# A different turn of gate quads, a later place for the transposes of u, earlier norms, and six weight tiles for five in a hybrid recurrence and retention layer

## The chip, the cores and the metric

The kernel runs on one core of a Trainium2 chip. The metric is device time in microseconds. The engines are TensorE (PE; its weight loads are PEld), VectorE (DVE), ScalarE (ACT), GpSimd (POOL) and SyncE (SP). Each works through its own instructions in order and waits for the others on semaphores. ACT, SP and POOL also issue DMA transfers; in the profile such issues stand under ACTq, SPq and POOLq.

## The reference

One layer over 2048 positions of width 1024, in float32:

```
h   = rms_norm(x) * (1 + scale(c)) + shift(c)
P   = h @ W_in         # 1024 x 9216: q f i z | q k v z | gA gB
uA  = headRMSNorm(HGRN2(q, f, i)) * silu(zA)
uB  = headRMSNorm(Retention(rot(q), rot(k), v)) * silu(zB)
m   = sigmoid(gA) * uA + sigmoid(gB) * uB
out = rms_norm(x + gate(c) * (m @ W_out))
```

Both branches have 8 heads. HGRN2 is a recurrence with a decay for each key channel: S_t = diag(f_t) S_(t-1) + (1 - f_t) i_t^T, o_t = S_t^T q_t. Retention has one fixed decay for each head and rotary positions on q and k.

## The kernel before

The sequence is worked on in two halves (superblocks) of 1024 positions, each as two blocks of 512. All columns of W_in for one head and purpose form a "quad": a 2 x 2 arrangement of two column groups by the two blocks. Each quad is computed by Strassen's scheme with Winograd's sums, so with seven products (numbered 1 to 7) in place of eight, and each product is four steps of three matmuls: every operand is split into a high and a low part in a reduced float32 format (fp32r), and high x high, high x low and low x high are added. A step is thus three matmuls of 128 x 512.

There are 36 quads in a half. Their names in the table ORDER are a (HGRN2 q and f of a head), v (both branches' values), b (retention q and k of a head pair), A and B (the gates zA with gA, and zB with gB, of a head). `product_order` interleaves the seven products of neighbouring quads: 2 of the new, 7 of the old, 1 and 5 of the new, 4 of the old, 3 and 6 of the new. PE's instructions are kept in the order in which the program writes them; the others are ordered by the scheduler, with priorities.

Results lie in PSUM banks: x0 and x1 in turn for a quad's x (and its y), v for products 5 and 3, lv, two of "o" and one double bank rt for the background. ACT copies y and v out of PSUM (L480); DVE adds or subtracts x (L493, L500, L504).

The raw weights come in tiles of 128 x 512 floats, with DMA issues on ACT's queue (L404), into a ring of NR tiles; DVE forms Winograd's sums in place (L419), and ACT and DVE split them (L293, L294) into the parts that PE reads, three products ahead. A new load is issued when a raw tile is done with.

Everything else is background: Python generators that issue a little work at each turn. `Background.tick` counts product steps; each 8 steps (GAP) all lanes get a turn (a burst), and each 4 steps the "side" generators do. The lanes are, for each head, the tree of score levels (bank lv, L70 with 128x16 and larger outputs, DVE L782 to L794), the HGRN2 output chunks (`hgrn_out`, banks poh), and for each head pair the retention chunks (`retention`, banks por and rt). Both end in `normed`: squares on ACT (L833), a power on POOL (L173 to L176), scaled copies on ACT (L836). The results u go to DRAM (L841). On the side run `next_h` (the normalized input of the second half) and, in the second half, `ada_row` (the gate row).

A quad A or B loads its u from DRAM (`fetch_u`, L670), turns it on PE by four transposes (`turned_u`, L73, tile uT) into bank v for the first block and into a used x bank for the second (`meet_last`), and DVE multiplies (L708). `fetch_u` demands that u has been stored for a while; where it has not, it issues bursts, one behind another, until it has.

`next_h` reads rows of x into two of the five shared temporaries (tag tp), squares them on ACT (L1038), adds on DVE (L1040), takes the power on POOL (L176), scales an identity on POOL (L1043, tile dgr), and has PE multiply by ones (tile rb); then it scales the transposed x. Rotary tables (ct, sn; issued on POOL's queue, L630 and L632) use the same temporaries, as do many results of DVE.

Of the kernel before, what the change touches and what calls it, by code (L numbers as in the profile page):

```python
# [9 lines left out]
F32 = mybir.dt.float32  # L10
# [12 lines left out]
P = 128  # L23
# [7 lines left out]
CH = SB // P  # L31
NA = 28
NBW = 3
NR = 5
NCC = 5
NTP = 5
NQP = 3
NVH = 2
GAP = 8.0
FIRST = 2  # L40


ORDER = """a0 v0 b0 v1 a1 b1 v2 a2 A0 B0 v3 a3 A1 B1 v4 b2 a4 A2 B2 v5 a5 A3 B3 v6 b3 a6 A4 B4 v7 a7 A5 B5 B6 A6 B7 A7"""


def all_quads():
# [3 lines left out]
QUADS = all_quads()  # L50
# [12 lines left out]
def tile_hybrid(ctx: ExitStack, tc: tile.TileContext, a: dict, out: bass.AP):  # L63
# [124 lines left out]
    class Background:  # L188

        def __init__(self):  # L190
            self.lanes = []
            self.side = []
            self.late = []
            self.since = 0.0
            self.beat = 0.0
            self.now = 0.0
            self.posts = []
# [41 lines left out]
        def tick(self, w):  # L239
            self.since += w  # L240
            self.beat += w
            self.now += w
            self.deliver()
            if self.beat >= 4.0:
                self.beat = 0.0
                self.aside()
            if self.since >= GAP:
                if self.burst():
                    self.since = 0.0

# [212 lines left out]
    def product_step(ps, m, q, j, first, last):  # L463
        sb = QUADS[q][0]
        at = combos[sb, ACOMBO[m], j]
        bt = W.parts[m, q]
        at_j = j % 2 * 2 + j // 2
        ls = [z[:, at_j * P : (at_j + 1) * P] for z in bt]
        for n, (x, y) in enumerate(((0, 0), (0, 1), (1, 0))):
            PE.matmul(  # L470
                out=ps, lhsT=ls[x], rhs=at[y], start=first and n == 0, stop=last and n == 2,
                skip_group_check=True,
            )
# [40 lines left out]
    def product(i):  # L514
        m, q = seq[i]
        if m == 2:
            ps = yb[q] = bank(f"y{q}", xtag(q))
        elif m == 1:
            ps = xb[q] = bank(f"x{q}", xtag(q))
        elif m == 5:  # L520
            ps = vb[q] = bank(f"v{q}", "v")
        elif m == 3:
            ps = vb[q]
        else:
            ps = xb[q]
        W.pump(i + NBW)
        for j in range(4):
            product_step(ps, m, q, j, m in (1, 2, 5) and j == 0, j == 3)
            bg.tick(1.0)
        W.parts.pop((m, q))  # L530
        after(m, q)
# [396 lines left out]
    def retention(p, sb):  # L928
# [26 lines left out]
        while n <= CH:  # L955
# [35 lines left out]
                        out=pos[j], lhsT=scms[m][:, j], rhs=vb_[j], start=g == 0, stop=True, skip_group_check=True  # L991
                    )
            if n < CH:
                scms[n] = upool.tile([P, 2, P], F32, name=f"scm{p}_{g0 + n}", tag="scm", bufs=2)
                V.tensor_tensor(out=scms[n], in0=pt[:, :, 0:P], in1=dT.rearrange("p (j t) -> p j t", j=2), op=ALU.mult)
                kzs[n] = upool.tile([P, P], F32, name=f"rkz{p}_{g0 + n}", tag="rkz", bufs=2)
                for j, r in enumerate(rows):
                    S.activation(out=kzs[n][:, r], in_=kz[:, r], func=AF.Copy, scale=zeta[:, h0 + j : h0 + j + 1])
            if n:
                if g and not last:  # L1000
                    V.scalar_tensor_tensor(
                        out=rs, in0=rs, scalar=gC[:, p : p + 1], in1=x, op0=ALU.mult, op1=ALU.add
                    )
                elif g == 0:
                    V.tensor_copy(out=rs, in_=x)
                b = g // 4
                if m % 2 == 0:
                    for j in range(2):
                        u[j] = upool.tile([P, 2, P], F32, name=f"ur{h0 + j}_{g}", tag="ur", bufs=4)
                normed(pos, [u[j][:, m % 2, :] for j in range(2)], f"r{p}_{g}", epsx[:, h0 : h0 + 2])  # L1010
                if m % 2:
                    for j in range(2):
                        send_u(1, h0 + j, b, m % 4, u[j])
                if m == CH - 1:
                    rnext[0] = (sb, p + 1) if p + 1 < NP else (sb + 1, 0)
                    if not last:
                        nc.sync.dma_start(out=rstd_d[p], in_=rs)
# [7 lines left out]
    def next_h(sb):  # L1025
        for tb in range(NBLK):
            b = sb * NBLK + tb
            rb = upool.tile([P, 512], F32, name=f"rb{b}", tag="mu", bufs=4)
            for t in range(4):
# [11 lines left out]
                rstd_of(r[:, 0:1], r[:, 0:1], D)  # L1041
                dg = tmp(f"dgr{b}_{t}", P)
                G.tensor_scalar(out=dg, in0=ident, scalar1=r[:, 0:1], scalar2=None, op0=ALU.mult)  # L1043
                yield
                yield
                ps = bank(f"rb{b}_{t}", "lv")
                PE.matmul(out=ps[:, 0:P], lhsT=ones, rhs=dg, start=True, stop=True)
                S.activation(out=rb[:, t * P : (t + 1) * P], in_=ps[:, 0:P], func=AF.Copy)
# [187 lines left out]
    def ada_row(j):  # L1236
# [9 lines left out]
                V.scalar_tensor_tensor(out=acc, in0=w, scalar=sc[:, kt : kt + 1], in1=acc, op0=ALU.mult, op1=ALU.add)  # L1246
        bgt = tmp(f"bg{j}")
        nc.sync.dma_start(out=bgt, in_=a["bgate"][:, j * 512 : (j + 1) * 512].broadcast_to([P, 512]))
        for _ in range(2):
            yield  # L1250
        ps = bank(f"gps{j}", "lv")
        PE.matmul(out=ps, lhsT=ones, rhs=acc, start=True, stop=True)
# [80 lines left out]
    for i in range(2, len(seq)):  # L1333
        m, q = seq[i]
        kind = QUADS[q][1]
        if m == 6 and 0 in waits:
            meet_last()
        if kind in "AB" and m == 6:
            turned_u(QUADS[q][2], "AB".index(kind), 0, "v")
        if kind in "AB" and m in (2, 1):  # L1340
            fetch_u(q, 2 - m)
        if kind == "b" and m == 2:
            load_rot(q, 0)
        if m == 2 and QUADS[q - 1][1] == "b":
            load_rot(q - 1, 1)
        if QUADS[q] == (0, "a", 5) and m == 1:
            bg.side.append(next_h(1))
        if QUADS[q] == (1, "a", 5) and m == 1:
            bg.side.append(chain(ada_row(0), ada_row(1)))
        if (m, q) == (1, mid):  # L1350
            pro["h"] = change_h(1)
# [130 lines left out]
```

## Time and profile before

| | |
|---|---|
| median of 3 runs | 2147.56 us (2147.33 to 2149.09) |
| the profiled execution | 2156.3 us, its span 2154.3 us |
| PE busy | 1978.3 us, 92% of the span |
| weight loads (PEld) | 1598.5 us, 74% |
| DVE busy | 1416.6 us, 66% |
| ACT busy | 995.0 us, 46% |
| POOL busy | 278.5 us, 13% |
| mean granted clock of TensorE | 0.966 |
| DMA | 259.95 MB in all, 121 GB/s on the mean |

In the page and in the answers of the trace, a line names a group of instructions or a stretch of time: a timeline row has start, duration, engine, line of the program, operation, out<-in (buffer numbers left out), the count, and in brackets the idle time before it and what ended it. A row of the table of stretches has start and end, length, the busy time of PE, PEld, DVE, ACT and POOL with their counts, the granted clock of TensorE as a share of full speed, the busy share of the 16 DMA engines, and GB/s. A row of the waits has the waiting engine, tile and line, the one waited for, the total, the times, and the longest. The chain is the work that ended last, followed back.

### The profile page before, as it was taken

To read this page: it belongs to the slowest core of one execution; us is meant where nothing else is said; L and a number is where in the kernel's file an instruction comes from. 1 tells how busy PE (TensorE), PEld (TensorE's weight loads), DVE (VectorE), ACT (ScalarE), POOL (GpSimd) and SP (SyncE) were. 2 spreads that over 40 slices of the span, in tenths; PEclk is the share of its full clock that TensorE was granted. 3 is DMA by queue.
4 is the path that set the end of the run, shared out by engine and by line. 5 is a ranking of instruction groups with operands and counts; after the bars stand their busy time and mean duration, and the time that the engine had idled before them with its cause. 6 is when DMAs were issued, how large, how long until landed. Compare 5 with 4: busy or idle time off the path is not lost.

```text
span 2154.3 us, 40023 instructions
## 1 busy us (share of the span) xinstructions
PE 1978.3 (92%) x15108; PEld 1598.5 (74%) x15108; DVE 1416.6 (66%) x2677; ACT 995.0 (46%) x2434; POOL 278.5 (13%) x514
## 2 busy tenths in 40 slices
PE   3889799998999879989998999999999899899998
PEld 2668587786777668768787788787777678687887
DVE  4876667675857557657876666676767576568432
ACT  5624444544355345445634445543454345444331
POOL 1001210211022110210002110211021101210000
PEclk9989999999999999989999999999999999899999
DMA  8145424352245536544544424352445324336442
GB/s 288 35 105 126 114 82 107 89 131 81 77 135 154 145 109 171 177 131 146 165 104 121 123 62 111 95 135 74 106 129 148 104 71 108 89 106 180 157 148 87
DMA packets 453120, 259.95 MB, mean 121 GB/s; under 512 B 171712, under 2 KB 406208, under 8 KB 452928
## 3 DMA queue, kind: packets, MB, share of 16 engines
q1 hardware_dynamic: 286752, 172.89, 28.6%
q10 hardware_dynamic: 153120, 76.04, 12.4%
q0 software_dynamic: 13056, 8.47, 1.5%
q8 instruction: 119, 1.95, 0.4%
q14 instruction: 73, 0.60, 0.1%
HBM read 188.03 MB, written 69.21 MB: 119 GB/s over the span
## 4 chain that ended last, share of the span: by engine, by line
PE 43%; DVE 7%; DMA 5%; ACT 4%; POOL 2%; issue 2%; ACTq 0%; SPq 0%; POOLq 0%; DVEq 0%
PE x L70 16%; PE v L70 8%; PE ops L70 8%; PE y L70 3%; DVE b L294 2%; PE lv L70 2%; PE poh L70 2%; PE rt L70 1%; DMA w<-in_w_d_dram 1%; ACT b L293 1%; DVE w L419 1%; PE uT L73 1%; PE por L70 1%; POOL rrh L176 1%; ACT c L480 1%
## 5 line engine op out<-in xcount | busy, mean ns | idle before, releaser
L294 DVE TENSOR_TENSOR b<-w,b 128x512 fp32r<-128x512 f32 (+1 forms) x553 | 346.5, 634 | 279.3 <-ACT b L293 273.7
L293 ACT ACTIVATE b<-w 128x512 fp32r<-128x512 f32 (+1 forms) x553 | 316.7, 583 | 289.6 <-PE x L70 210.2
L70 PE MATMUL x<-A,b 128*128 128x512 f32 x1704 | 429.8, 401 | 12.4 <-ACT c L480 11.5
L70 PE MATMUL v<-S,b 128*128 128x512 f32 x1704 | 429.8, 401 | 8.5 <-ACT c L480 6.0
L70 PE MATMUL x<-S,b 128*128 128x512 f32 x1704 | 431.6, 403 | 1.6 <-DVE c L500 0.9
L70 PEld LDWEIGHTS x<-A,b 128*128 128x128 f32 x1704 | 321.5, 192 | 81.8 <-ACT c L480 12.6
L70 PEld LDWEIGHTS v<-S,b 128*128 128x128 f32 x1704 | 322.0, 192 | 79.7 <-ACT c L480 8.7
L70 PEld LDWEIGHTS x<-S,b 128*128 128x128 f32 x1704 | 321.5, 193 | 68.2 <-DVE c L500 1.3
L419 DVE TENSOR_TENSOR w<-w,w 128x512 f32<-128x512 f32 x284 | 195.1, 687 | 62.7 <-DMA w<-in_w_a_dram 24.4
L70 PE MATMUL y<-A,b 128*128 128x512 f32 x840 | 209.1, 398 | 8.6 <-DVE vt L592 8.6
L70 PEld LDWEIGHTS y<-A,b 128*128 128x128 f32 x840 | 156.9, 190 | 41.8 <-issue 7.4
L70 PE MATMUL ops<-wo,m 128*128 128x512 f32 x768 | 174.8, 389 | 0.0
L70 PEld LDWEIGHTS ops<-wo,m 128*128 128x128 f32 x768 | 144.0, 188 | 30.2 <-DVE m L299 0.4
L173 POOL TENSOR_SCALAR ssh<-ssh 128x1 f32<-128x1 f32 x128 | 44.9, 351 | 845.0 <-ACT uh L833 841.7
L480 ACT ACTIVATE c<-v 128x512 f32<-128x512 f32 x142 | 84.5, 595 | 121.7 <-PE v L70 106.9
L836 ACT ACTIVATE uh<-poh,rrh 128x128 f32<-128x128 f32 x128 | 47.1, 368 | 125.1 <-POOL rrh L176 123.7
L70 PEld LDWEIGHTS lv<-q,k 128*32 128x32 f32 (+1 forms) x5888 | 71.0, 110 | 43.9 <-issue 27.8
L70 PE MATMUL lv<-q,k 128*32 128x16 f32 (+2 forms) x5888 | 82.5, 189 | 18.9 <-DVE ad L794 6.2
L500 DVE TENSOR_TENSOR c<-c,x 128x512 f32<-128x512 f32 x71 | 48.7, 687 | 76.7 <-PE x L70 76.5
L782 DVE TENSOR_TENSOR q<-q,f 128x512 f32<-128x512 f32 x112 | 76.9, 687 | 22.6 <-PE lv L70 22.2
L176 POOL TENSOR_TENSOR rrh<-ssh,mhalf 128x1 f32<-128x1 f32 x128 | 84.0, 656 | 10.4
L783 DVE TENSOR_TENSOR k<-k,f 128x512 f32<-128x512 f32 x112 | 77.1, 688 | 0.0
(191 smaller groups left out, 2409.3 us busy)
## 6 DMA issues: line engine op xcount, KB each, us to landing
w<-in_w_d_dram ACTq DMA_DIRECT2D x128, 256.0 KB
w<-in_w_c_dram ACTq DMA_DIRECT2D x66, 256.0 KB
mu<-ud SPq DMA_DIRECT2D x64, 256.0 KB
w<-in_w_a_dram ACTq DMA_DIRECT2D x60, 256.0 KB
wa<-in_w_ada_dram SPq DMA_DIRECT2D x16, 512.0 KB
w<-in_w_b_dram ACTq DMA_DIRECT2D x32, 256.0 KB
vd<-vt SPq DMA_DIRECT2D x128, 64.0 KB
vdr<-vt SPq DMA_DIRECT2D x128, 64.0 KB
```

Source lines behind the costliest of these rows:

```text
L70: return tc.keep_in_program_order(nc.tensor.matmul(**kw))
L73: return tc.keep_in_program_order(nc.tensor.transpose(**kw))
L173: G.tensor_scalar(out=ss, in0=ss, scalar1=n * EPS, scalar2=None, op0=ALU.add)
L176: G.tensor_tensor(out=dst, in0=ss, in1=mhalf.broadcast_to([P, w]), op=ALU.pow)
L293: S.activation(out=t[0], in_=src, func=AF.Copy)
L294: return V.tensor_tensor(out=t[1], in0=src, in1=t[0], op=ALU.subtract)
L419: V.tensor_tensor(out=out, in0=x, in1=y, op=ALU.add)
L480: S.activation(out=t, in_=ps, func=AF.Copy)
L500: V.tensor_tensor(out=t, in0=t, in1=xb[q], op=ALU.subtract)
L782: V.tensor_tensor(out=qv, in0=qv, in1=tv[:, :, :, 0:1].broadcast_to([P, NU, nb, m]), op=ALU.mult)
L783: V.tensor_tensor(out=kv, in0=kv, in1=tv[:, :, :, 1:2].broadcast_to([P, NU, nb, m]), op=ALU.mult)
L836: S.activation(out=dsts[i], in_=pos[i], func=AF.Copy, scale=rr[:, i : i + 1])
```

## The change

It has these parts:

- the transposes of a gate quad's first block (into v) are issued inside product 6, after its second step, where they stood ahead of product 6 before;
- in ORDER, v7 stands ahead of A4 and B4, and A6 ahead of B6;
- from quad B6 on the burst gap is 4 steps, and 8 again from the second half's a0 on (GAP_OF);
- `next_h` and `ada_row` start at v4 rather than a5; the matmul for rb comes four side turns after its scaling rather than two, and the one for the gate row five turns after the last load rather than two;
- the ring of raw weight tiles has six rather than five;
- the masked scores (scm) and the scaled keys (rkz) of the retention have one buffer rather than two, and its u tiles (ur) three rather than four.

```diff
-NR = 5
+NR = 6
...
 GAP = 8.0
 FIRST = 2
+GAP_OF = {("B", 6): 4.0, ("a", 0): GAP}
...
-ORDER = """a0 v0 b0 v1 a1 b1 v2 a2 A0 B0 v3 a3 A1 B1 v4 b2 a4 A2 B2 v5 a5 A3 B3 v6 b3 a6 A4 B4 v7 a7 A5 B5 B6 A6 B7 A7"""
+ORDER = """a0 v0 b0 v1 a1 b1 v2 a2 A0 B0 v3 a3 A1 B1 v4 b2 a4 A2 B2 v5 a5 A3 B3 v6 b3 a6 v7 A4 B4 a7 A5 B5 A6 B6 B7 A7"""
...
-            if self.since >= GAP:
+            if self.since >= self.gap:
                 if self.burst():
                     self.since = 0.0
...
         for j in range(4):
+            if m == 6 and j == 2 and QUADS[q][1] in "AB":
+                turned_u(QUADS[q][2], "AB".index(QUADS[q][1]), 0, "v")
             product_step(ps, m, q, j, m in (1, 2, 5) and j == 0, j == 3)
...
-                scms[n] = upool.tile([P, 2, P], F32, name=f"scm{p}_{g0 + n}", tag="scm", bufs=2)
+                scms[n] = upool.tile([P, 2, P], F32, name=f"scm{p}_{g0 + n}", tag="scm", bufs=1)
...
-                kzs[n] = upool.tile([P, P], F32, name=f"rkz{p}_{g0 + n}", tag="rkz", bufs=2)
+                kzs[n] = upool.tile([P, P], F32, name=f"rkz{p}_{g0 + n}", tag="rkz", bufs=1)
...
-                        u[j] = upool.tile([P, 2, P], F32, name=f"ur{h0 + j}_{g}", tag="ur", bufs=4)
+                        u[j] = upool.tile([P, 2, P], F32, name=f"ur{h0 + j}_{g}", tag="ur", bufs=3)
...
                 G.tensor_scalar(out=dg, in0=ident, scalar1=r[:, 0:1], scalar2=None, op0=ALU.mult)
-                yield
-                yield
+                for _ in range(4):
+                    yield
                 ps = bank(f"rb{b}_{t}", "lv")
...
-        for _ in range(2):
+        for _ in range(5):
             yield
         ps = bank(f"gps{j}", "lv")
...
-        if kind in "AB" and m == 6:
-            turned_u(QUADS[q][2], "AB".index(kind), 0, "v")
...
+        if m == 2:
+            bg.gap = GAP_OF.get(QUADS[q][1:], bg.gap)
...
-        if QUADS[q] == (0, "a", 5) and m == 1:
+        if QUADS[q] == (0, "v", 4) and m == 1:
             bg.side.append(next_h(1))
-        if QUADS[q] == (1, "a", 5) and m == 1:
+        if QUADS[q] == (1, "v", 4) and m == 1:
             bg.side.append(chain(ada_row(0), ada_row(1)))
```

Three places show how instructions move. Line numbers of the changed kernel are one to four higher for the same statement.

The first is PE at the end of the first half, where u of head 6 is asked for. Quad 31 is B5 in both; quad 32 is B6 before and A6 now; lv, kT and poh7 are the tree, the transposed keys and the output chunks of head 7, por3 and rt3 the retention of heads 6 and 7. Before:

```order
L70 MATMUL lv7_0_16_9606<-q7_0_8605,k7_0_8604 16x16 x32
L70 MATMUL por3_8_9649<-rs3_0_8725,rqk3_7_9457 128x128
L70 MATMUL rt3_8_9648<-rs3_0_8725,rqk3_7_9457 128x128
L70 MATMUL rt3_8_9648<-vr3_7_9577,rkz3_7_9592 64x128 x2
L70 MATMUL por3_8_9649<-vr3_7_9577,scm3_7_9590 128x128
L70 MATMUL rt3_8_9648<-vr3_7_9577,scm3_7_9590 128x128
L70 MATMUL lv7_0_32_9666<-q7_0_8605,k7_0_8604 32x32 x16
L70 MATMUL lv7_0_64_9694<-q7_0_8605,k7_0_8604 64x64 x8
L73 MATMUL kT7_0_0_9712<-ident_74,k7_0_8604 128x128 x4
L73 MATMUL kT7_0_1_9721<-ident_74,k7_0_8604 128x128 x4
L70 MATMUL poh7_0_9739<-vh7_0_0_9399,k7_0_8604 128x128
```

And now, from the same level of the tree on:

```order
L71 MATMUL lv7_0_16_9659<-q7_0_8812,k7_0_8811 16x16 x32
L71 MATMUL x32_9703<-A11_0_0_304,b1_32_9625 128x512 x3
L71 MATMUL x32_9703<-A11_0_1_409,b1_32_9625 128x512 x3
L71 MATMUL x32_9703<-A11_0_2_487,b1_32_9625 128x512 x3
L71 MATMUL x32_9703<-A11_0_3_587,b1_32_9625 128x512 x3
L71 MATMUL v32_9725<-S1_0_0_517,b5_32_9642 128x512 x3
L71 MATMUL v32_9725<-S1_0_1_617,b5_32_9642 128x512 x3
L71 MATMUL v32_9725<-S1_0_2_697,b5_32_9642 128x512 x3
L71 MATMUL v32_9725<-S1_0_3_735,b5_32_9642 128x512 x3
L71 MATMUL lv7_0_32_9741<-q7_0_8812,k7_0_8811 32x32 x16
```

The run of 25 such rows without a product between them (its middle is shown) is gone; the tree's levels stand two products apart, and the retention's last chunks stand further ahead.

The second is ACT at the quad v1 (quad 3; quad 4 is a1, quad 5 is b1; wN_0 to wN_3 are the four raw tiles of quad N). Before:

```order
L404 DMA w4_2_1325<-in_w_a_dram 128x4x128
L293 ACTIVATE b3_3_1343<-w3_3_1166 128x512
L404 DMA w4_0_1390<-in_w_a_dram 128x4x128
L480 ACTIVATE c5_3_1382<-v3_1342 128x512
L293 ACTIVATE b6_3_1384<-w3_0_1086 128x512
```

And now:

```order
L406 DMA w4_0_1327<-in_w_a_dram 128x4x128
L295 ACTIVATE b3_3_1345<-w3_3_1090 128x512
L406 DMA w4_1_1392<-in_w_a_dram 128x4x128
L482 ACTIVATE c5_3_1384<-v3_1344 128x512
L295 ACTIVATE b6_3_1386<-w3_0_998 128x512
```

The issues stand at the same places among ACT's instructions, and each asks for the next tile in the line.

The third is POOL at quad b2 (quad 15): ct and sn are the rotary tables, xr and dgr belong to the norms of `next_h`. Before:

```order
L176 TENSOR_TENSOR rrr1_7_4564<-ssr1_7_4563,mhalf_79 128x2
L630 DMA ct15_0_4734<-lin_230 128x1x512
L632 DMA sn15_0_4735<-lin_230 64x1x512 x2
L630 DMA ct15_1_4951<-lin_230 128x1x512
L632 DMA sn15_1_4952<-lin_230 64x1x512 x2
L173 TENSOR_SCALAR ssh3_0_5003<-ssh3_0_5003 128x1
```

And now:

```order
L177 TENSOR_TENSOR rrr1_7_4572<-ssr1_7_4571,mhalf_79 128x2
L174 TENSOR_SCALAR xr2_0_4652<-xr2_0_4652 128x1
L177 TENSOR_TENSOR xr2_0_4652<-xr2_0_4652,mhalf_79 128x1
L1047 TENSOR_SCALAR dgr2_0_4656<-ident_74,xr2_0_4652 128x128
L634 DMA ct15_0_4750<-lin_230 128x1x512
L636 DMA sn15_0_4751<-lin_230 64x1x512 x2
L174 TENSOR_SCALAR xr2_1_4895<-xr2_1_4895 128x1
L177 TENSOR_TENSOR xr2_1_4895<-xr2_1_4895,mhalf_79 128x1
L1047 TENSOR_SCALAR dgr2_1_4899<-ident_74,xr2_1_4895 128x128
```

The norms of the first two row groups stand before and between the loads of the two tables; before, they came some five quads later.

More of the change, by code (lines that the diff above doesn't have):

```diff
@@ L194, in __init__ @@
             self.since = 0.0
+            self.gap = GAP
             self.beat = 0.0
```

## The prediction

> **What bounds the kernel now.** I read the page's busy table first, then the stretches, then the table of waits of TensorE (PE), then the timeline around the longest ones.
>
> ```profile
> PE 1978.3 (92%) x15108; PEld 1598.5 (74%) x15108; DVE 1416.6 (66%) x2677; ACT 995.0 (46%) x2434; POOL 278.5 (13%) x514
> ```
>
> PE is the bound; VectorE (DVE) and ScalarE (ACT) have room on average, so they cost only where a PE instruction waits for one. In the stretches view the columns are start and end, length, PE, PEld, DVE, ACT and POOL busy, granted clock, DMA share, GB/s.
>
> ```profile
> 107.00:2040.00 1933.00, 1806.67 (x14325) 1462.72 (x14324) 1306.03 (x2468) 899.52 (x2267) 258.73 (x466) 0.97 0.43 118
> 970.00:1065.00 95.00, 92.98 (x427) 76.51 (x426) 75.58 (x124) 55.87 (x104) 4.88 (x9) 1.00 0.51 161
> ```
>
> I measure what a stretch loses as length minus PE busy times clock: the idle time plus what a slow clock stretched. From 107 to 2040 us that is 1933 - 1806.67 x 0.97 = 181 us, 9.3%. From 970 to 1065, where products run nearly alone, it is 2.0 us, 2%. So the products are not the problem; what the background steps and the evictions do to PE is. Who is waited for (total, times, longest):
>
> ```profile
> PE uT L73 <- ACT c L480: 30.1, 20, 4.5
> PE x L70 <- ACT c L480: 12.2, 4, 5.9
> PE rb L70 <- POOL dgr L1043: 9.2, 2, 6.2
> PE gps L70 <- DVE acc L1246: 4.8, 1, 4.8
> PE rb L70 <- DVE ad L794: 3.3, 1, 3.3
> ```
>
> **The change, part by part.** *Turns.* The four transposes of a gate quad (uT into bank v) stand right behind the product that ended in v, so they wait until ACT has copied v out (L480). The worst case, and the chain's price of 24 products' matmuls:
>
> ```profile
> 908.26 0.60 PE L73 MATMUL uT<-ident,mu 128*128 128x128 f32 x4
> 913.33 0.78 PE L73 MATMUL uT<-ident,mu 128*128 128x128 f32 x4 [4.46 <-ACT c L480]
> 990.20 5.44 PE x L70 x24
> 629.19 0.66 PE L73 MATMUL uT<-ident,mu 128*128 128x128 f32 x4 [2.49 <-ACT c L480]
> 628.00:635.00 7.00, 5.81 (x27) 4.53 (x29) 1.63 (x4) 2.34 (x7) 1.68 (x3) 0.76 0.59 170
> ```
>
> A matmul takes 5.44 / 24 = 0.227 us; the change puts six of them ahead, 1.36 us of cover that needs no copy of v. Of the 20 waits 11 are shorter than 1.36 us (6.2 us together) and go; 9 are longer and lose 1.36 us each, 12.2 us. That is 18.4 of 30.1 us; the 4.46 us wait keeps 3.1. The clock: after 2.49 us of waiting, 628 to 635 ran at 0.76 and lost 7 - 5.81 x 0.76 = 2.6 us, of which 1.2 is the wait's own end, so 1.4 is clock. Six of the waits are of that length or near it, up to 8 us; since the long ones only shrink, I take 3. Term: **21** (15 to 27). By the Trainium skill, "TensorE: Matmul & The Clock Gate", Part 1, the clock drops after about 3.4 us of idleness; only the three longest waits would then have cost clock, all three would fall below that length, and the term would be 18.4 + 3 x 1.4 = 23. The 2.49 us row disagrees: it is shorter and cost clock.
>
> The transposes end before the product does, and the multiplication that reads them needs that product, so it is not late.
>
> *Last quads.* Before, the load of u for B6 finds the retention of heads 6 and 7 unfinished, and eleven rounds of background are issued with no product between them, in both halves. They depend on each other through DVE, ACT and POOL:
>
> ```profile
> 928.80:948.70 19.90, 10.47 (x84) 8.43 (x84) 9.18 (x22) 7.92 (x30) 4.95 (x8) 0.57 0.40 129
> 1865.80:1884.50 18.70, 10.15 (x88) 8.48 (x84) 6.64 (x16) 7.86 (x30) 3.53 (x8) 0.63 0.26 78
> 930.74 0.78 PE L70 MATMUL por<-rs,rqk 64*128 64x128 f32 x2 [1.93 <-DVE rs L1001]
> 934.49 0.79 PE L70 MATMUL rt<-rs,rqk 64*128 64x128 f32 x2 [2.97 <-ACT ur L836]
> 948.04 0.49 PE L70 MATMUL poh<-vh,k 128*128 128x128 f32 x2 [0.87 <-ACT uh L836]
> ```
>
> Loss: 19.9 - 10.47 x 0.57 = 13.9 and 18.7 - 10.15 x 0.63 = 12.3, together 26.2 us. With v7 ahead of A4 the retention starts two quads sooner, and in the changed order every such round has products around it: the run of 25 background rows is gone and the longest left is 12, as elsewhere before. Against it: from B6 on rounds come every 4 product steps, not 8. That is 12 matmuls, 2.7 us, per output chunk of head 7, 16 chunks; the one wait of that kind here was 0.87 us, so 0 to 14 us; with two banks I take 4. Term: **22** (12 to 26). A6 ahead of B6 by itself moves no work.
>
> *Norms and gate rows.* The sum-of-squares matmul (rb) gets 16 product steps after its scaling, not 8; gps gets five turns, not two. These are the four places (three rb, then gps):
>
> ```profile
> 736.00:744.00 8.00, 5.04 (x17) 3.77 (x16) 2.06 (x5) 3.86 (x8) 3.06 (x6) 0.79 0.77 219
> 753.00:765.00 12.00, 5.76 (x21) 4.39 (x20) 3.58 (x8) 3.88 (x11) 3.05 (x5) 0.72 0.38 123
> 789.00:798.00 9.00, 5.68 (x63) 3.89 (x65) 4.78 (x11) 2.68 (x5) 0.00 (x0) 0.81 0.28 76
> 1680.00:1690.00 10.00, 5.23 (x15) 3.24 (x14) 5.07 (x9) 2.26 (x4) 1.30 (x2) 0.83 0.70 163
> 756.51 0.63 ACT L1038 ACTIVATE xt<-xt 128x512 f32<-128x512 f32 x1 [7.01 <-DMA xt<-in_x_dram]
> 759.94 0.80 PE L70 MATMUL rb<-dgr,ones 128*128 128x128 f32 x2 [6.24 <-POOL dgr L1043]
> ```
>
> Losses 4.0, 7.9, 4.4 and 5.7, together 22 us. The added 8 steps are 24 matmuls, 5.44 us, more than two of the three rb waits and nearly the third. But the cause stays: ACT stood 7.01 us at the square (L1038), whose load takes a turn in the five shared temporaries together with the rotary tables of b3. Starting at v4 moves the first block's squares from a5 to b2, where tables are loaded as well, and an ACT that stands there holds up evictions whatever rb does. POOL's rb steps now also stand around the loads of b2. I take **9** (-10 to 22).
>
> *Six raw tiles.* Weights are added on DVE as soon as their load has landed; these are late:
>
> ```profile
> 724.76 0.69 DVE L419 TENSOR_TENSOR w<-w,w 128x512 f32<-128x512 f32 x1 [6.04 <-DMA w<-in_w_a_dram]
> 1174.74 0.69 DVE L419 TENSOR_TENSOR w<-w,w 128x512 f32<-128x512 f32 x1 [5.18 <-DMA w<-in_w_c_dram]
> 1710.90 0.69 DVE L419 TENSOR_TENSOR w<-w,w 128x512 f32<-128x512 f32 x1 [6.03 <-DMA w<-in_w_d_dram]
> 1701.34 9.47 DMA w<-in_w_d_dram
> 1701.30:1710.90 9.60, 7.10 (x34) 5.48 (x32) 2.15 (x4) 3.42 (x8) 1.37 (x2) 1.00 0.39 117
> 724.00:734.00 10.00, 6.56 (x21) 5.32 (x22) 6.62 (x12) 4.09 (x10) 1.46 (x2) 0.66 0.41 126
> 1172.00:1184.00 12.00, 6.15 (x32) 4.25 (x30) 9.20 (x20) 4.01 (x15) 2.68 (x4) 0.72 0.18 47
> 1704.00:1717.00 13.00, 9.15 (x39) 7.15 (x38) 6.21 (x11) 3.06 (x9) 2.16 (x4) 0.87 0.27 80
> ```
>
> PE loses 5.7, 7.6 and 5.0 us behind them, 18 us: DVE waits, ACT waits for DVE, the copy of y or x queues behind. One tile more asks for each load one load earlier. The page counts 286 weight loads (128 + 66 + 60 + 32), one per 1933 / 286 = 6.8 us on average, more than each of the three waits. Where releases come close together the lead is shorter, so **12** (0 to 18).
>
> *Single buffers* (scm, rkz) and three ur tiles for four. The new masked scores must wait for the old ones' matmuls:
>
> ```profile
> 919.70 0.39 PE L70 MATMUL rt<-vr,scm 128*128 128x128 f32 x2
> 920.36 0.42 DVE L995 TENSOR_TENSOR scm<-rt,dT 128x256 f32<-128x256 f32 x1
> 256.31 0.81 SPq L841 DMA_DIRECT2D ud<-ur  x2
> 262.14 0.28 ACT L833 ACTIVATE ur<-rt 128x128 f32<-128x128 f32 x1 [0.26 <-DVE rs L1001]
> ```
>
> DVE already starts scm after the last matmul that reads the old one (both use bank rt), so it costs 0 while that order holds; rkz is written later still. If the cover went, it would be 64 waits of some 1.3 us on DVE, with a third of its time free. The ur tile's reuse comes 5.83 us after its store is issued; I count 0, at worst a few us.
>
> *What no row shows*: the waits that a new order makes itself. The background losses outside the four terms are 181 - 38 - 26 - 22 - 18 = 77 us (38 is the turns' 30 and 8), spread over the whole program; I take **-4** (0 to -20).
>
> Sum: 21 + 22 + 9 + 12 - 4 = 60 us. The profiled execution is 2156.3 us (span 2154.3 and 2.0 around it), 8.7 above the median of 2147.56; the saved time is waits, the same in either, so 2156.3 becomes 2096 and the median **2088**.
>
> **The rivals.**
>
> A, the stalls only move. ACT is in order, and what makes v late is its queue (squares, then copies that wait for POOL), not the place of the transposes; behind a late ACT the next product waits for bank x instead, as the 12.2 us row shows. Then the turns give 6 (the short waits), the weights 4, the norms nothing: 22 + 6 + 4 - 4 = 28, so 2120. For it: 3.1 us of the 4.46 remain. Against: the banks alternate, so x has a product more time. 0.17.
>
> B, the sixth load does not land sooner. By the Trainium skill, "DMA: Bandwidth & Descriptors", Queues, rings and completion order, each engine takes packets from the queue rows in turn, so one more load in flight shares the same engines. Worked from the rows: were the engines full while a load is late, its term would be 0 and the time 2100. They are 0.39 busy from 1701.30 to 1710.90, which speaks for latency, not for a full engine. 0.09.
>
> C, slower: the squares at b2. If each of the eight squares of the norms finds its load late as at 756.51, PE loses the 753 to 765 stretch's 7.9 us eight times, 63 us, against 21 + 22 + 12 = 55 from the rest: 2156. It decides from about seven such stalls. Against it: before, rb made PE wait three times at eight sums, and the stretch that the squares move into asks less of the DMA engines than the one they leave:
>
> ```profile
> 646.00:970.00 324.00, 288.88 (x2390) 232.37 (x2389) 214.80 (x417) 157.12 (x408) 53.90 (x95) 0.94 0.51 148
> 430.00:646.00 216.00, 203.41 (x1575) 164.73 (x1575) 141.71 (x270) 101.81 (x264) 30.30 (x57) 0.98 0.39 105
> ```
>
> 0.09.
>
> D, all terms at their upper end, 27 + 26 + 22 + 18 = 93: 2055. 0.07.
>
> **How the numbers follow.** The forecast has 0.58, its own range 2070 to 2108. A measurement of this kernel cannot tell 0.2%, 4.3 us, from no change. A's upper part (0.03) and C's lower (0.01) fall there. Faster 0.88, same 0.04, slower 0.08. Range 2058 to 2130, with D's last part and C outside.
>
> **What would show it.** The uT row of the waits falls to about 12 us, none over 3.2. No PE stretch like 928 to 948 remains, and rounds around B6 wait under 1 us each. rb and gps leave the table, or shrink below 3 us, and ACT's wait for xt appears near b2, under 8 us. DVE's waits of 5 to 6 us for w loads are gone. The 107 to 2040 loss drops from 181 to about 120 us. I am wrong if that loss stays above 160: then ACT or POOL sets the waits, wherever PE's instructions stand.

## The result, and the profile after

| | before | after |
|---|---|---|
| median, us | 2148.32 | 2066.97 (2062.72 to 2069.38) |
| ratio | | 0.9615, 95% interval 0.959 to 0.9639 |
| profiled execution, its span, us | 2156.3, 2154.3 | 2069.4, 2067.6 |
| mean granted clock | 0.966 | 0.982 |

The change made the kernel faster by 83 us by the ratio (0.0385 x 2148.32; interval 78 to 88). The forecast was 60 us, to 2088, in a range of 2058 to 2130: the time lies in the range, and the gain was put 23 us too small. It lies 3 us below 2070 to 2108, the range that the prediction gave its own theory; the wider range holds it because it also takes in the slower part of rival D. The experiments ask which term of the sum was too small.

The page's busy row of the kernel after has the same instructions as before in 30.3 us less of PE's time (1948.0 for 1978.3); of the 86.7 us by which the span is shorter, the other 56.4 are idle time of PE:

```profile
PE 1948.0 (94%) x15108; PEld 1578.1 (76%) x15108; DVE 1411.8 (68%) x2677; ACT 993.2 (48%) x2434; POOL 271.8 (13%) x514
```

The same stretch as the prediction's first row, of the kernel after, and the stretches of the last quads of both halves, where the forced rounds stood (columns as there: start and end, length, PE, PEld, DVE, ACT and POOL busy, clock, DMA share, GB/s):

```profile
107.00:2040.00 1933.00, 1864.71 (x14708) 1515.06 (x14707) 1332.38 (x2519) 922.67 (x2320) 258.81 (x482) 0.99 0.45 125
880.00:975.00 95.00, 93.29 (x739) 76.83 (x738) 67.72 (x126) 44.95 (x103) 11.11 (x22) 1.00 0.33 97
1800.00:1885.00 85.00, 82.85 (x446) 68.45 (x447) 64.24 (x109) 42.83 (x92) 7.31 (x16) 1.00 0.41 124
```

The loss from 107 to 2040 us is 1933 - 1864.71 x 0.99 = 87 us, where it was 181 and 120 was forecast (the clock is printed to 0.01, so this is good to about 9 us). In the last quads PE loses next to nothing, 1.7 and 2.2 us.

PE's waits from 107 to the span's end, of the kernel after (who waits, for whom, total, times, longest):

```profile
PE lv L71 <- DVE ad L798: 10.8, 7, 2.8
PE v L71 <- ACT c L482: 10.7, 5, 4.6
PE y L71 <- DVE vt L596: 8.6, 2, 7.1
PE x L71 <- ACT c L482: 5.8, 2, 3.2
PE uT L74 <- ACT c L482: 2.9, 3, 2.2
PE rb L71 <- POOL ssr L176: 0.6, 1, 0.6
```

The uT row has gone from 30.1 us to 2.9, rb from 12.5 to 0.6, gps has left the table. Some rows rose: v from 5.3 to 10.7, lv<-DVE ad from 6.2 to 10.8, uT<-DVE sz from 0.7 to 3.7, and y<-ACT uh is new with 3.6. All rows together are 68 us, 126 before.

Now DVE. Its waits for raw weights from 107 us on in the kernel before; the prediction showed three of the five longest single ones, 17 us, and not these rows:

```profile
DVE w L419 <- DMA w<-in_w_a_dram: 24.4, 8, 6.0
DVE w L419 <- DMA w<-in_w_d_dram: 22.1, 7, 6.0
DVE w L419 <- DMA w<-in_w_b_dram: 6.8, 3, 3.6
DVE w L419 <- DMA w<-in_w_c_dram: 5.2, 1, 5.2
```

These are 58.5 us in 19 waits. After, two are left:

```profile
DVE w L421 <- DMA w<-in_w_d_dram: 1.7, 1, 1.7
DVE w L421 <- DMA w<-in_w_b_dram: 0.2, 1, 0.2
```

### The profile page after: what moved, and what is told of

Read it like the earlier page. It is cut to its first block, busy times and chain, and to the rows that moved or that the text cites. A ratio compares the mean times of both kernels' runs of the same rounds, so it can differ in the third digit from the quotient of the medians.

```text
span 2067.6 us, 40051 instructions
## 1 busy us (share of the span) xinstructions
PE 1948.0 (94%) x15108; PEld 1578.1 (76%) x15108; DVE 1411.8 (68%) x2677; ACT 993.2 (48%) x2434; POOL 271.8 (13%) x514
## 4 chain that ended last, share of the span: by engine, by line
PE 39%; DVE 5%; DMA 5%; ACT 2%; issue 1%; POOL 1%; SPq 0%; ACTq 0%; POOLq 0%; DVEq 0%
PE x L71 14%; PE ops L71 8%; PE v L71 7%; PE y L71 3%; PE poh L71 1%; DVE b L296 1%; PE lv L71 1%; DMA ud<-ur 1%; PE rt L71 1%; DMA wg<-in_w_gate_dram 1%; DVE w L421 1%; PE uT L74 1%; PE por L71 1%; ACT b L295 1%; DMA rd<-ro 1%
## 5 line engine op out<-in xcount | busy, mean ns | idle before, releaser
L71 PE MATMUL v<-S,b 128*128 128x512 f32 x1704 | 429.2, 401 | 11.6 <-ACT c L482 11.3
L71 PE MATMUL x<-A,b 128*128 128x512 f32 x1704 | 425.3, 397 | 6.6 <-ACT c L482 5.8
L71 PEld LDWEIGHTS x<-S,b 128*128 128x128 f32 x1704 | 312.1, 189 | 64.6 <-DVE b L296 2.0
L71 PE MATMUL lv<-q,k 128*32 128x16 f32 (+2 forms) x5888 | 80.5, 187 | 21.6 <-DVE ad L798 10.8
L176 POOL TENSOR_TENSOR ssr<-ssr,epsx 128x2 f32<-128x2 f32 x64 | 20.9, 326 | 458.7 <-ACT ur L837 458.6
```

What stands on the lines that cost most here:

```text
L71: return tc.keep_in_program_order(nc.tensor.matmul(**kw))
L176: G.tensor_tensor(out=ss, in0=ss, in1=eps, op=ALU.add)
```

## The experiments

All kernels compute the whole layer. S is the theory on record. A gain or loss against the kernel before is (1 - ratio) x the median of the runs of before that stood beside it (2148 to 2153 us). Where a kernel is compared with the changed one, it is the difference of the two ratios to before times 2150 us, and its half-width is that of both ratios in quadrature, 6.5 to 8 us.

### The turns alone

```diff
         for j in range(4):
+            if m == 6 and j == 2 and QUADS[q][1] in "AB":
+                turned_u(QUADS[q][2], "AB".index(QUADS[q][1]), 0, "v")
             product_step(ps, m, q, j, m in (1, 2, 5) and j == 0, j == 3)
...
-        if kind in "AB" and m == 6:
-            turned_u(QUADS[q][2], "AB".index(kind), 0, "v")
```

> The kernel before with the turns alone: the four transposes of a gate quad's first block stand behind the second step of product 6. Theory on record (S): the cover is 1.36 us, so of the 30.1 us that the transposes wait for the copy of v, 11 short waits go and 9 long ones lose 1.36 us each; the uT row falls to about 12 us, longest 3.1, and the time by 21 us (15 to 27), to about 2127. Rival L, from the trace after, where the row is 2.9 us in 3 waits: the early place itself ends nearly all of these waits, since what keeps ACT late is undone as well when PE goes on; row at most 4 us, time down 30 us or more, to 2118 or less. Rival M: the long waits went after because other parts of the change took their cause away; here they stay, row 10 us or more, and the time falls by no more than S says. Rival A: they move to x; the row x<-ACT c rises from 12.2 us by as much as uT falls, gain 6 us.

Measured: 2132.48 us (2126.88 to 2136.07), ratio 0.9919 (0.9905 to 0.9934): 17 us saved (14 to 20). PE's waits of this kernel:

```profile
PE x L70 <- ACT c L480: 12.1, 3, 5.8
PE uT L73 <- ACT c L480: 11.3, 7, 2.5
```

S said 12 us for the uT row and 11.3 stand there; 20 waits have become 7. The row x<-ACT c, where rival A sent the waits, is 12.1 (12.2 before). So A falls. L falls too, and M is right on one point: the rest of the uT row, from 11.3 to the 2.9 of the kernel after, went through other parts. The profiled execution of this kernel lies 29 us below that of the kernel before and the medians 18, so rows of two profiles are not good to the last few us.

### The last quads alone

```diff
+GAP_OF = {("B", 6): 4.0, ("a", 0): GAP}
...
-... b3 a6 A4 B4 v7 a7 A5 B5 B6 A6 B7 A7"""
+... b3 a6 v7 A4 B4 a7 A5 B5 A6 B6 B7 A7"""
```

> The kernel before with the last quads alone: v7 ahead of A4 and B4, A6 ahead of B6, and a gap of 4 steps from B6 on. S: both runs of eleven rounds without a product go (26 us of loss), dense rounds take 4 back: 22 us (12 to 26), to about 2126; the uT row stays near 30 us. Rival L: the dense rounds cost nothing: 26 us or more, to 2122 or less. If the early v7 also takes away uT waits (the longest, 4.46 us, stood at 913, just ahead of the forced rounds), the uT row falls by 5 to 10 us and the gain is over 30.

Measured: 2128.68 us (2124.16 to 2130.84), ratio 0.9897 (0.9882 to 0.9912): 22 us saved (19 to 25), S's number. The two stretches that hold the last quads, first of the kernel before, then of this one:

```profile
880.00:970.00 90.00, 75.84 (x744) 61.44 (x743) 57.71 (x117) 40.26 (x124) 19.61 (x32) 0.89 0.45 139
1800.00:1895.00 95.00, 85.65 (x817) 69.49 (x816) 55.09 (x114) 48.77 (x150) 20.00 (x38) 0.93 0.30 89
```

```profile
880.00:970.00 90.00, 85.11 (x761) 70.14 (x761) 66.66 (x130) 42.54 (x99) 10.83 (x20) 0.98 0.48 147
1800.00:1895.00 95.00, 91.32 (x796) 75.20 (x794) 64.48 (x122) 45.71 (x113) 12.19 (x24) 0.98 0.28 83
```

Before they lose 22.5 and 15.3 us, 38 together, of which the two forced bursts are 26; with the last quads turned, 90 - 85.11 x 0.98 = 6.6 and 95 - 91.32 x 0.98 = 5.5, 12 together. From the end of one product's matmul to the start of the next, the longest pieces of PE's timeline are 22.3 us (from 926.4) and 20.9 us (from 1863.5) before; now no piece in the last quads is longer than 3.6 us. The uT row is 28.8: the early v7 takes next to nothing from it. L's 26 us or more are not reached. Whether the early v7 or A6 ahead of B6 does it was not tried one by one.

### The norms and gate rows alone

```diff
-                yield
-                yield
+                for _ in range(4):
+                    yield
                 ps = bank(f"rb{b}_{t}", "lv")
...
-        for _ in range(2):
+        for _ in range(5):
             yield
         ps = bank(f"gps{j}", "lv")
...
-        if QUADS[q] == (0, "a", 5) and m == 1:
+        if QUADS[q] == (0, "v", 4) and m == 1:
...
-        if QUADS[q] == (1, "a", 5) and m == 1:
+        if QUADS[q] == (1, "v", 4) and m == 1:
```

> The kernel before with the norms and gate rows alone: next_h and ada_row start at v4 (not a5), and rb and gps come four and five side turns behind (not two). S: of the 22 us that PE loses at the four places, 9 are saved (-10 to 22), since ACT stands at the squares near b2 instead: to about 2139. Rival L, from the trace after, where rb has 0.6 us in one wait and gps none: all of the 22 us go, and the stand of ACT near b2 (3.4 and 2.2 us in the trace after) costs up to 5: 17 to 22 us, to 2126 to 2131. Rival C: the squares at b2 make it slower than before.

Measured: 2147.01 us (2141.29 to 2154.93), ratio 0.9982 (0.9967 to 0.9998): 4 us saved (0.4 to 7). rb and gps, 17.3 us of waits before, are out of the table, but (waits, and the timeline where the largest new one begins; a timeline row has start, duration, engine, line, operation, count, and in brackets the idle time before it and what ended it):

```profile
PE v L70 <- ACT c L480: 19.6, 9, 6.9
```

```profile
1450.17 0.69 DVE L643 TENSOR_TENSOR sw<-c,sn 64x512 f32<-64x512 f32 x1 [5.14 <-DMA sn<-lin]
1453.97 0.60 ACT L480 ACTIVATE c<-v 128x512 f32<-128x512 f32 x1 [7.26 <-DVE c L645]
1454.62 1.65 PE L70 MATMUL v<-S,b 128*128 128x512 f32 x3 [6.87 <-ACT c L480]
```

The waits for v have risen from 5.3 to 19.6 us. In the second half the gate row's loads now run with the rotary tables of b2 and share their temporaries: the table sn comes late, DVE stands 5.14 us for it, ACT's copy waits for DVE, PE for the copy. A late weight is part of the same chain: POOL issued sn at 1440.73 us, after 5.14 us of waiting for DVE, and DVE had just stood 4.53 us for a raw weight (1439.14). In the changed kernel PE's wait for v at this place is 4.77 us with five weight tiles (1436.59) and 0.89 with six (1430.86). That the shared temporaries are a cause is read from this chain; no run gave the gate rows temporaries of their own. The gain at one place was spent at another. C falls, since the part is not slower, and so does L with its 17 to 22 us.

### Six raw weight tiles alone

```diff
-NR = 5
+NR = 6
...
-tag="scm", bufs=2
+tag="scm", bufs=1
...
-tag="rkz", bufs=2
+tag="rkz", bufs=1
...
-tag="ur", bufs=4
+tag="ur", bufs=3
```

> The kernel before with six raw weight tiles and, as the room for the sixth demands, single scm and rkz and three ur tiles. S: DVE's waits of 5 to 6 us for late weight loads go, 12 us (0 to 18) saved, the single buffers cost 0: to about 2136. Rival B: the sixth load lands no sooner: same time as before, DVE's waits of 5 to 6 us stay. Rival U, from the trace after, where ACT waited 7.0, 2.1 and 1.7 us for the stores of ur: the sixth tile is worth up to 18, but three ur tiles take 5 to 8 back; then the waits for w are gone and ACT waits for ud<-ur appear, with a gain of 5 to 12.

Measured: 2113.85 us (2110.84 to 2119.8), ratio 0.9836 (0.9819 to 0.9853): 35 us saved (32 to 39). This is the largest of the four parts, and three times what S gave it. No theory stated had it above 18; the waits for a ur tile's store that U named are there, 4.1 us in two, but U's gain of 5 to 12 is not. The page's group of the weight sums in this kernel, with its idle time (62.7 us before), and PE's waits:

```profile
L419 DVE TENSOR_TENSOR w<-w,w 128x512 f32<-128x512 f32 x284 | 195.0, 687 | 4.5 <-DMA w<-in_w_c_dram 0.6
```

```profile
PE uT L73 <- ACT c L480: 23.1, 19, 3.9
PE rt L70 <- ACT ur L836: 6.0, 3, 3.3
PE x L70 <- ACT c L480: 3.6, 2, 2.1
```

The 58.5 us of DVE's waits for weights are gone, so rival B falls. On PE's side the gain stands under other names: uT<-ACT c 7.0 us less than before, x<-ACT c 8.6 less, rt<-ACT ur 3.3 less. How a late weight comes to stand under ACT is seen in the kernel before:

```profile
1174.74 0.69 DVE L419 TENSOR_TENSOR w<-w,w 128x512 f32<-128x512 f32 x1 [5.18 <-DMA w<-in_w_c_dram]
1177.32 0.28 ACT L833 ACTIVATE ur<-rt 128x128 f32<-128x128 f32 x1 [9.98 <-DVE rs L1001]
1177.84 0.60 ACT L480 ACTIVATE c<-y 128x512 f32<-128x512 f32 x1
1178.49 1.65 PE L70 MATMUL x<-A,b 128*128 128x512 f32 x3 [5.85 <-ACT c L480]
```

DVE stands for the weight, the state rs of the retention is queued behind it, ACT stands 9.98 us for rs (5.18 of them are DVE's wait), the copy of y is queued behind that, and PE waits for the copy. By the table of waits PE waits for ACT; the cause is a load, two engines away. Of the span's 42.9 us (2154.3 to 2111.4), 27 are PE's waits (126 to 99) and most of the rest is PE's own time: 14.2 us less busy for the same instructions, at a clock of 0.975 for 0.966.

### The single buffers alone

```diff
-tag="scm", bufs=2
+tag="scm", bufs=1
...
-tag="rkz", bufs=2
+tag="rkz", bufs=1
...
-tag="ur", bufs=4
+tag="ur", bufs=3
```

> The kernel before with only the single buffers: one scm and one rkz for two, three ur tiles for four, five raw weight tiles as before. S: 0, the same time as before. Rival U: the three ur tiles cost 5 us or more, since ACT then waits for their stores (7.0, 2.1 and 1.7 us for ud<-ur in the trace after); the sixth tile's own worth would be so much above the 35 us of the run with both.

Measured: 2151.09 us (2145.42 to 2156.34), ratio 1.0004 (0.9989 to 1.0019): S's 0 holds, to 4 us, and U's loss of 5 us or more falls. DVE still waits for weights:

```profile
DVE w L419 <- DMA w<-in_w_a_dram: 22.3, 7, 6.0
DVE w L419 <- DMA w<-in_w_d_dram: 21.0, 7, 6.0
```

So the 35 us of the run before belong to the sixth tile.

### The changed kernel with five tiles

```diff
-NR = 6
+NR = 5
```

> The changed kernel with five raw weight tiles (single buffers and all else as changed). S: 12 us above the changed kernel. Theory W, from the run with six tiles alone (35 us for 58.5 us of DVE's waits for weights in 19 places, of which S counted three): 30 to 37 us above it, near 2100, and DVE's waits for w are back with 50 us or more. Rival X: in the changed order the waits fall on other places and part of what the tile saved is saved by the turns or the quads as well; then 15 to 28 us.

Measured: 2104.88 us (2101.97 to 2111.11), ratio to the kernel before 0.9795 (0.9774 to 0.9816): 39 us above the changed kernel. Theory W holds, X and S fall. DVE's waits of this kernel are back with 67.8 us, and so is the row x<-ACT c of PE:

```profile
DVE w L421 <- DMA w<-in_w_a_dram: 28.1, 7, 6.1
DVE w L421 <- DMA w<-in_w_d_dram: 14.5, 9, 4.2
DVE w L421 <- DMA w<-in_w_b_dram: 14.1, 6, 4.7
DVE w L421 <- DMA w<-in_w_c_dram: 11.1, 2, 6.2
```

```profile
PE x L71 <- ACT c L482: 12.7, 3, 6.6
PE uT L74 <- ACT c L482: 7.4, 5, 2.2
```

Both ways the price is the same: 35 us for 58.5 us of such waits, and 39 for the 65.9 that come back (67.8 less 1.9), 0.6 us of the program for each.

### The changed kernel with the turns back

The `turned_u` lines of the first experiment, moved back ahead of product 6.

> The changed kernel with the transposes of the first block back ahead of product 6. S: 21 us above the changed kernel. Theory W, that the parts share their causes: six tiles alone took 7 us and the norms alone 8 us from the 30.1 us of uT's waits, so some 15 remain here; 10 to 15 us above it, near 2080. Rival N: no sharing, 17 us or more, as with the turns alone.

Measured: 2090.68 us (2086.41 to 2094.9), ratio to before 0.9718 (0.9692 to 0.9744): 22 us above the changed kernel, +- 8. S's 21 holds, and N, that the parts don't share; W's upper end, 15 us, is just inside the interval and not excluded.

```profile
PE uT L74 <- ACT c L482: 23.0, 19, 3.6
```

The other parts leave 23.0 of the 30.1 us, as many as six tiles alone did (23.1). The early place takes 18.8 us from the row alone (30.1 to 11.3) and 20.1 here (23.0 to 2.9).

### The changed kernel with the norms back

Start at a5, two turns ahead of rb and of gps.

> The changed kernel with next_h and ada_row started at a5 again and with two side turns ahead of rb and gps again. S: 9 us above the changed kernel. Theory T: 4 us, as the part saved alone, with rb and gps back at 12 to 18 us in PE's waits and v<-ACT c down from 10.7 to 5. Rival K: behind six tiles the norms are worth more, 10 us or more, since without late weights rb's waits are what is left in that stretch.

Measured: 2070.08 us (2065.06 to 2071.88), ratio to before 0.9616 (0.9594 to 0.9637): the same as the changed kernel, within 7 us. K's 10 us or more and S's 9 fall; T's 4 us cannot be told from 0. The waits of PE for rb and gps:

```profile
PE rb L71 <- POOL dgr L1047: 9.0, 2, 4.6
PE gps L71 <- DVE acc L1250: 4.8, 1, 4.8
PE rb L71 <- DVE ad L798: 2.8, 1, 2.8
```

rb and gps are back with 16.6 us, and v<-ACT c is down to 0.9. Counted by the starts of the products' matmuls in the two profiled executions (5952 in each), this kernel is ahead of the changed one by 2 us at the 1200th and by 9 at the 1300th, where the changed kernel waits for v near 491 us. The lead is 14 us at the 4200th (near 1378) and 20 at the 4450th (near 1449), and falls to 5 by the 5250th (near 1679): 15 us go around gps. So the norms' part costs time near b2 in both halves and wins it back at gps; at rb, near 700 to 800 us, it wins little that this count shows.

### Other starts for the norms and the gate rows

```diff
-        if QUADS[q] == (0, "v", 4) and m == 1:
+        if QUADS[q] == (0, "a", 4) and m == 1:
...
-        if QUADS[q] == (1, "v", 4) and m == 1:
+        if QUADS[q] == (1, "a", 4) and m == 1:
```

That is the first; the second has a4 and v4, the third a4 and v2.

> The changed kernel with next_h and ada_row started at a4, two quads later, so past b2, whose rotary tables take turns in the same temporaries; the longer gaps for rb and gps stay. Theory T: what the norms' part gives back (the run with it alone saved 4 us although rb and gps, 17 us, were gone; PE's waits for v rose from 5 to 20 us) is the stand of ACT at b2, so the waits of v near 490 and 1440 go, and the time falls by 5 to 10 us below the changed kernel, to about 2060. Rival V: the stalls follow the norms to where they go (b3 lies 11 quads on, and the second block then meets it), same time within 3 us. Rival R: with the later start rb's and xT's loads meet b3 as they did before: slower by 5 or more.

> The changed kernel with next_h started at a4 (past b2) and ada_row at v4 as changed: the half of the earlier run with both at a4 that stood ahead of the changed kernel (3 us at the end of the first half by the products' starts), without the one that lost (12 us between products' steps 4400 and 4600, near 1410 to 1466). Theory P: the two halves are independent, 2 to 6 us below the changed kernel, near 2062. Rival Q: such differences are the spread of single executions (the changed kernel's own runs lie 2062.7 to 2069.4), within 2 us of it.

> The changed kernel with next_h at a4 and ada_row at v2, so that the gate row's loads lie behind b1's tables and end before b2's. Theory P: PE's waits near 1437 (uT 2.2, and what stands around it) go as well, 4 to 9 us below the changed kernel, near 2059. Rival Q: within 2 us of it. Rival V: the loads slow other work in v2 to v3, where two HGRN2 heads are in the background: slower by 3 or more.

Measured: 2072.55 us (ratio 0.9642, 0.9624 to 0.9659), 2069.51 (0.9607, 0.958 to 0.9634) and 2070.49 (0.9622, 0.9599 to 0.9645). Against the changed kernel that is +6, -2 and +2 us, +- 6.5, 8 and 7. None is faster beyond doubt. T falls; for a4 in both halves R is nearest, but V is not excluded. The two others are nearest to Q, but their intervals are too wide to exclude P, nor V for the third. The waits moved: with a4 and a4 the 4.65 us wait for v near 491 is gone, and PE waits for the HGRN2 state at another place, behind a DVE that stood 7.43 us for a gate weight (1413.84); with a4 and v2 DVE stands for a gate weight as well, elsewhere (two pieces of the timelines, one of each kernel):

```profile
1415.50 0.80 PE L71 MATMUL poh<-st,q 128*128 128x128 f32 x2 [5.04 <-DVE st L910]
```

```profile
1170.34 0.75 DVE L1250 SCALAR_TENSOR_TENSOR acc<-wg,sc,acc 128x512 f32<-128x512 f32 x1 [7.68 <-DMA wg<-in_w_gate_dram]
1171.84 1.62 PE L71 MATMUL x<-S,b 128*128 128x512 f32 x3 [9.99 <-DVE c L502]
```

### The changed kernel with a gap of 8

```diff
-GAP_OF = {("B", 6): 4.0, ("a", 0): GAP}
+GAP_OF = {}
```

> The changed kernel with a gap of 8 steps throughout, the order of the quads as changed. S charged the dense rounds 4 us and took it that the order alone takes the forced rounds away: 0 to 4 us faster than the changed kernel. Rival G: head 7's output chunks are then not done when A7 and B7 ask for its u, and rounds are forced there: 10 us or more slower, and a stretch of PE near the end of each half with rounds and no products.

Measured: 2074.11 us (2072.18 to 2076.83), ratio to before 0.9649 (0.9631 to 0.9667): 7 us above the changed kernel, +- 6.5. The last quads of this kernel:

```profile
880.00:975.00 95.00, 93.55 (x768) 77.45 (x757) 70.83 (x130) 43.41 (x96) 9.77 (x16) 1.00 0.31 96
1800.00:1885.00 85.00, 80.10 (x402) 65.83 (x402) 61.68 (x105) 40.92 (x90) 9.19 (x16) 1.00 0.40 120
```

There are no forced rounds here either (no piece of the last quads without a product is longer than 4.7 us), so G's mechanism falls: the order alone takes them away. S's 0 to 4 us faster falls too; if the gap of 4 does anything in the changed kernel, it helps. In the second half this kernel loses 4.9 us to the changed kernel's 2.2. Where the rest of the 7 us lies, the two profiles don't say (their spans differ by 2.8 us), and it stays open.

## Why the prediction was right, and what was mis-sized

| term | on record | alone | taken out of the changed kernel |
|---|---|---|---|
| turns | 21 (15 to 27) | 17 (14 to 20) | 22 +- 8 |
| last quads | 22 (12 to 26) | 22 (19 to 25) | |
| norms, gate rows | 9 (-10 to 22) | 4 (0.4 to 7) | 0 +- 7 |
| six tiles | 12 (0 to 18) | 35 (32 to 39) | 39 +- 7 |
| single buffers (also in the row above) | 0 | -1 (-4 to 2) | |
| what no row shows | -4 (0 to -20) | | |
| sum | 60 | 78 (17 + 22 + 4 + 35) | 83 measured together |

**Six tiles** is the term that was mis-sized: 12 on record, 35 to 39 measured. The mechanism was right: each load is asked for one load earlier, DVE's waits go. The failing step was the price. The prediction took three waits of the timeline, "PE loses 5.7, 7.6 and 5.0 us behind them, 18 us", and called that the whole; the table of DVE's waits had 19 of them with 58.5 us. Sixteen waits of 0.3 to 6 us, 41 us together, were priced at nothing, although two were nearly as long as the longest shown (5.97 and 5.98 us at 252.83 and 511.41). The upper bound of 18 was thus no bound. Had the term been worked out from the grouped row, even at 0.6 us for each (the price that the runs show, known only now), it would have been 35, and the sum 83. That this meets the measured 83 is in part luck, since the turns and the norms gave less than their terms. A third of the 18 was then taken off for "where releases come close together", which the runs don't show either: 1.9 us of waits are left.

There was a second way to see it. Part of the loss that the prediction booked elsewhere was late weights that stand under ACT: the rows uT, x and rt lost 19 us when the sixth tile came (7.0 + 8.6 + 3.3). Of these, 7.0 were inside the turns' 30.1, and some of the rest in the 77 us of background "spread over the whole program".

**Turns**: right, by size and by row. 11.3 us left in the uT row where "about 12" was worked out, the longest 2.5 where 3.1 was. In the kernel after it is 2.9 in three waits; with five tiles there it is 7.4 and with the norms back 3.8, so the sixth tile does most of the rest.

The clock was charged 3 us, taken from up to 8. PE's busy time fell by 10.7 us with the turns alone, so this was rather too little, though the two profiles lie further apart than the medians. Whether a wait costs clock is not decided by its length alone. In the kernel after, PE waited 2.20 us up to 988.08 and 2.19 us up to 1437.42 (both for uT), and only the first is followed by a lower clock. Stretches of 3.41 us, the length for which the clock stayed low there, show where each wait lies:

```profile
985.32:988.74 3.42, 1.22 (x8) 0.80 (x7) 1.59 (x4) 2.04 (x4) 0.00 (x0) 1.00 0.95 307
988.74:992.15 3.41, 3.41 (x11) 2.73 (x11) 3.41 (x6) 3.04 (x7) 0.00 (x0) 0.50 0.62 188
1435.90:1439.31 3.41, 1.89 (x11) 1.63 (x12) 1.92 (x5) 1.37 (x3) 0.57 (x1) 1.00 0.44 146
1439.31:1442.72 3.41, 3.41 (x19) 2.92 (x18) 2.60 (x6) 1.52 (x4) 0.09 (x1) 1.00 0.28 77
```

The first wait lies whole in one stretch (3.42 - 1.22 = 2.20 us idle), and the next stretch runs at 0.50 (from 992.15 on it is 1.00 again). The second is split on the same grid: 0.67 us lie in the stretch from 1432.48 and 1.52 in the one from 1435.90, and the clock stays at 1.00. By the Trainium skill, "TensorE: Matmul & The Clock Gate", Part 1, the activity is watched in a free-running window, so two equal waits can fall differently in it; that agrees with these rows. A threshold at 3.4 us of one wait does not: 2.20 us were enough here, and in the kernel before the 2.49 us wait, 2.18 of it in the stretch 627.01 to 630.42, was followed by 0.50 up to 633.84.

**Last quads**: right, 22. The order takes the forced rounds away. At the place itself the loss fell by 26 us (38 to 12), as much as the bursts lost and with the dense rounds in it, so the 4 us charged for these don't show there; the whole program gained 22, and where the other 4 went stays open. The number is thus in part lucky.

**Norms**: the mechanism that was feared, C's, was seen, but far smaller than C had it. rb and gps cost next to nothing any more (17.3 us of waits before, 0.6 after), and ACT and DVE stand for loads near b2 instead, as this piece of the kernel after shows (ACT first, then PE):

```profile
483.47 0.63 ACT L1042 ACTIVATE xt<-xt 128x512 f32<-128x512 f32 x1 [3.37 <-DMA xt<-in_x_dram]
491.56 5.49 PE L71 MATMUL v<-S,b 128*128 128x512 f32 x12 [4.65 <-ACT c L482]
```

The term was 9 within wide bounds and is 0 to 4. It was not the squares alone: in the run of this part alone the largest new wait came in the second half, where the gate row's loads and the rotary table met, with a late weight in the same chain.

**What no row shows**: -4 was charged; the parts alone add to 78 (17 + 22 + 4 + 35, the single buffers being in the 35) against 83 together, so the new order made no loss that can be seen (the interval of 83 is 78 to 88, and the sum of four runs is known to about 7). New waits there were all the same, and one came through the ur ring, which was counted at 0: in the kernel after, ACT stands 10.8 us in three waits for a store to free a ur tile, the longest 7.0, and PE waited 2.5 us for x behind the longest (ACT's row of waits, and a timeline row of PE):

```profile
ACT ur L837 <- DMA ud<-ur: 10.8, 3, 7.0
```

```profile
1137.94 0.96 PE L71 MATMUL x<-A,b 128*128 128x512 f32 x3 [2.54 <-ACT c L482]
```

With the single buffers alone this row is 1.9. It does not follow the speed: the changed kernel with the norms back, as fast, has 3.9, with the turns back 4.0 and with a gap of 8 3.5, none with a wait over 2.1. What makes the wait of 7.0 stays open.

**The rivals.** A (the stalls move to x): no, 12.1 for 12.2 with the turns alone; it had the norms at nothing, which is near what they gave. B (the sixth load lands no sooner): no. C: not slower. D had the turns, quads, norms and tiles at 27, 26, 22 and 18, sum 93; its time, 2055, is 12 us from the result and so nearer to the result than the forecast's 2088, but for the wrong reason, since the gain came from the term that D capped at 18.

**What would show it.** The PE stretch without products is gone (the waits in the last quads are at most 1.5 us, where under 1 was named), rb and gps left, ACT's wait for xt appeared near b2 (3.37 us, under the 8 named), DVE's weight waits are gone, the loss fell below 160, as named. It fell to 87 (+- 9) instead of 120; most of the difference is the weights' term, 23 to 27 us above its 12.

## What to carry to other kernels

Price a stall from the row that groups it over the whole program, not from a few cases in the timeline: the waits left out were 41 of 58.5 us here. Look for the cause where an in-order engine stands for a load, even when the table of waits of the bound engine names another engine; every instruction queued behind it hands the wait on. When two streams of loads share a few temporaries, moving one of them earlier moves the stall, and only the run says which place is cheaper.

## What the runs showed of the hardware that was not expected

A third of the gain is not idle time. With the same 15108 matmuls PE was busy 30.3 us less (1978.3 to 1948.0) while its mean granted clock rose from 0.966 to 0.982; the kernel with six tiles alone had 14.2 us of this, the turns alone 10.7 (1967.6). Busy time x mean clock is the same before and after, 1911 and 1913 us, so the clock accounts for the 30.3, to a few us (the mean clock is taken over the whole span, not over the busy time). The prediction counted the clock only in the stretches just behind long waits, 3 us for the turns. Over these four kernels one with fewer waits of PE also spent less time in the same matmuls: 126 us of waits and 1978.3 busy before, 99 and 1964.1 with six tiles, 83 and 1953.1 with the turns back, 68 and 1948.0 after. Among the kernels near 70 us of waits this order no longer holds (1944.3 busy with 73 us of waits in the one with a4 and v2).
